# Repeated bias rows copied DRAM to DRAM in sixteen pieces, behind a modulation that begins one group earlier

## The chip, the cores and the metric

The kernel runs on one core of a Trainium2 chip. The metric is device time in microseconds for one execution; the time before is the median of three runs. The core has five engines that run instruction queues of their own: TensorE (PE, with its weight loads as PEld), VectorE (DVE), ScalarE (ACT), GpSimd (POOL) and SyncE (SP), which here issues all the DMAs. Every queue is worked off in order; an instruction that waits for a semaphore holds back what stands behind it on the same engine. The DMAs themselves run on sixteen DMA engines.

## The reference, cut to what matters

One layer of a streaming encoder on 1024 prompt frames and 32 sample frames, width 1024, in fp32:

```python
mod = jax.nn.silu(c) @ w_mod + b_mod                       # 9 vectors of 1024: shift, scale, gate for 3 sub-layers
h = adaln_in(x, gains[0], sh1, sc1)
x = x + 0.5 * g1 * rmsnorm(swiglu(h, w1_gate, w1_up, w1_down), gains[1])      # d_ff 2816
...
bias_a = rel_tab_a[:, clip(k - q, -128, 128) + 128]        # 8 heads
bias_b = t5_tab[:, t5_bucket(k - q)]                       # 8 heads
... attention with these biases, output projection, gate g2, then a second swiglu with g3
```

The change concerns two things that are needed late: the modulation vectors from number 2 on (first used when the first SwiGLU is complete), and the two bias tables, which the attention adds to its scores.

## The kernel before, in words

The first SwiGLU (`ffn("h1", ...)`, lines 516 to 597) works in 11 groups of two blocks of 128 hidden columns, x and y. For each of three blocks of frames (384, 384 and 288) a group computes `gate` and `up` for x and for y (24 matmuls of three terms for each product, in PSUM banks of which three rotate), the activation `sl` (ScalarE L541), its product with `up` (VectorE L542), a split into two parts `gg` (L544, L545) and the down projection `dn` of both, which is added to `facc` (L570, L572). The down projection of one block of frames runs between x and y of the next. The last three groups run their third block of frames at the end.

Every weight block of 512 KB is loaded by a DMA into `raw` (L292; three buffers, shared with the modulation's loads), and split there into two parts: ScalarE rounds it (L294), VectorE subtracts (L295). The loads for a group are issued during the group before it. ScalarE's splits stand in its queue between the `sl` of the running group, so a load that lands late holds back the next `sl`, and with it a PSUM bank that TensorE needs.

Side work is written as generators. `step(n)` runs the next pieces of the queue `side` and is called from inside the groups. The modulation is such a generator: `mod_aside(n)` (L215) loads one of 14 remaining chunks in four DMAs (L220), multiplies and adds on VectorE (L227, L229), and transposes the sums on TensorE into `pmt` (L239), which VectorE reduces into `modT` (L240). `mod_rest(gi)` (L625) is called at the end of group gi. After group 0 it called `bias_rows()` all at once; after group 1 it began the modulation.

`bias_rows()` (L251) loads both tables (L253, L258), lays each out on eight partitions, one head each, as 384 values (`ua`, `ubt`; 31 small copies at L261 for the second), and copies them to DRAM, each head's row 128 times over (L265): `skew_A` and `skew_B`, 8 x 128 x 384 values or 1.5 MB each. `bias_tiles` (L276) later reads them with a row step of 383 instead of 384, which shifts each row by one.

The order in which the DMAs stand on SyncE, and the instructions on the other engines, comes from a scheduler that simulates times while the program is built (from the end of group 0 on, for SyncE). DMAs use eight completion semaphores in turn, so one may have to wait for an earlier one that used the same.

Of the kernel before, what the change touches and what calls it, by code (L numbers as in the profile page):

```python
# [7 lines left out]
F32 = mybir.dt.float32  # L8
# [66 lines left out]
def encoder_step(ctx: ExitStack, tc, x_prompt, x_sample, cache_a_k, cache_a_v, cache_b_k, cache_b_v,  # L75
# [4 lines left out]
    te, ve, ae, ge, dma = nc.tensor, nc.vector, nc.scalar, nc.gpsimd, nc.sync  # L80
# [12 lines left out]
    dram = ctx.enter_context(tc.tile_pool(name="dram", bufs=1, space=DRAM))  # L93
# [12 lines left out]
    def s_tile(shape, name, dt=F32):  # L106
        return spool.tile(shape, dt, name=name, tag="s")
# [107 lines left out]
    def mod_aside(n):  # L215

        acc = [h_tile([128, 512], "macc") for _ in range(2)]
        for g in range(4):
            r = rpool.tile([128, 2, 512], F32, name="raw", tag="r")
            dma.dma_start(r, w_mod[0, 256 * g:256 * (g + 1), 512 * n:512 * (n + 1)]  # L220
                          .rearrange("(k p) n -> p k n", p=128))
            for kk in range(2):
                k = 2 * g + kk
                for j in range(2):
                    c = csil[:, k, j:j + 1]
                    if k == 0:
                        ve.tensor_scalar(acc[j], r[:, kk], c, None, op0=OP.mult)  # L227
                    else:
                        ve.scalar_tensor_tensor(acc[j], r[:, kk], c, acc[j], op0=OP.mult, op1=OP.add)  # L229
            yield  # L230
            yield
            yield
        yield
        yield
        c0 = 4 * n
        for j in range(2):
            pt = pc("pmt", (128, 4, 128))
            for b in range(4):
                te.transpose(pt[:, b, :], acc[j][:, 128 * b:128 * b + 128], ident)  # L239
            ve.tensor_reduce(modT[:, j, c0:c0 + 4], pt, axis=AX.X, op=OP.add)  # L240
        coefs(n)
        yield

    def mod_all(first, last):
        for n in range(first, last):
            yield from mod_aside(n)


    ub = {}

    def bias_rows():  # L251
        ta = s_tile([8, 257], "ta")
        dma.dma_start(ta, rel_bias_a[0])  # L253
        ua = s_tile([8, 384], "ua")
        ve.memset(ua[:, 0:128], 0.0)
        ve.tensor_scalar(ua[:, 128:384], ta[:, 0:256], ta[:, 0:1], None, op0=OP.subtract)
        tt = s_tile([8, 32], "tt")
        dma.dma_start(tt, t5_bias_table)  # L258
        ubt = s_tile([8, 384], "ubt")
        for lo, hi, b in T5_RANGES:  # L260
            ve.tensor_copy(ubt[:, lo + 255:hi + 256], tt[:, b:b + 1].to_broadcast([8, hi - lo + 1]))  # L261
        ve.memset(ubt[:, 383:384], 0.0)
        for kind, u in (("A", ua), ("B", ubt)):
            ub[kind] = dram.tile([8, 128, 384], F32, name="skew_" + kind)
            dma.dma_start(ub[kind], u[:, None, :].to_broadcast([8, 128, 384]))  # L265
        sk = consts.tile([128, 8], F32, name="sk")
        dma.dma_start(sk, bass.AP(tensor=sinks_b.tensor, offset=sinks_b.offset, ap=[[0, 128], [1, 8]]))
        sks = consts.tile([64, 4], F32, name="sks")
        for h in range(2):
            dma.dma_start(sks[32 * h:32 * h + 32], bass.AP(tensor=sinks_b.tensor, offset=sinks_b.offset + h,  # L270
                                                          ap=[[0, 32], [2, 4]]))
        nsk = consts.tile([128, 8], F32, name="nsk")
        ve.tensor_scalar(nsk, sk, -1.0, None, op0=OP.mult)
        ub["sk"], ub["sks"], ub["nsk"] = sk, sks, nsk
# [210 lines left out]
    def begin(key, gen, first=False):  # L485
        side.insert(0 if first else len(side), marked(key, gen))

    def marked(key, gen):
        yield from gen
        done.add(key)  # L490
# [5 lines left out]
    def between(f, tb, j, H):  # L496
        yield from resid(f, tb, j)
        dma.dma_start(xs_dram[j + 1][tb], f)
        yield from norm_h(f, tb, j + 1, H)
# [125 lines left out]
    def mod_rest(gi):  # L625
        if gi == 0:
            in_order.close()
            bias_rows()
        if gi == 1:
            begin("mod", mod_all(4, 18))  # L630

    ffn1 = ffn("h1", H1, F1, w1_gate, w1_up, w1_down, mod_rest, "h2", lambda tb: between(F1[tb], tb, 0, H2))
    first = start(0)
    for o in START:
# [713 lines left out]
```

## Time and profile before

| | |
|---|---|
| runs | 2225.36, 2229.99, 2230.26 us; median 2229.99 |
| the profiled execution | 2232.07 us, span 2230.3 us |
| mean granted clock of TensorE in it | 0.983 |
| busy in the span | TensorE 2163.1 us (97%), VectorE 1238.6 (56%), ScalarE 698.1 (31%), GpSimd 180.5 (8%) |
| DMA | 186.00 MB, mean 83 GB/s |

The first SwiGLU takes the time from 46 to about 840 us, the attention follows, and the second SwiGLU ends the program. To read it: TensorE is the engine that is busy nearly throughout, so the other engines' idle time says little by itself. What counts is where TensorE idles, who ended that, and at which clock it then runs. The groups can be told apart by the `sl` activations, six to a group; the first one (x, first frames) of groups 1 to 3 is at 124.25, 207.01 and 278.71 us.

### The profile page before, as it was taken

To read this page: it belongs to the slowest core of one execution; us is meant where nothing else is said; L and a number is where in the kernel's file an instruction comes from. 1 tells how busy PE (TensorE), PEld (TensorE's weight loads), DVE (VectorE), ACT (ScalarE), POOL (GpSimd) and SP (SyncE) were. 2 spreads that over 40 slices of the span, in tenths; PEclk is the share of its full clock that TensorE was granted. 3 is DMA by queue.
4 is the path that set the end of the run, shared out by engine and by line. 5 is a ranking of instruction groups with operands and counts; after the bars stand their busy time and mean duration, and the time that the engine had idled before them with its cause. 6 is when DMAs were issued, how large, how long until landed. Compare 5 with 4: busy or idle time off the path is not lost.

```text
span 2230.3 us, 33962 instructions
## 1 busy us (share of the span) xinstructions
PE 2163.1 (97%) x14012; PEld 2069.8 (93%) x14012; DVE 1238.6 (56%) x2425; ACT 698.1 (31%) x1450; POOL 180.5 (8%) x281
## 2 busy tenths in 40 slices
PE   6989999999999999899999899999999999999998
PEld 4989999999999999899788579999999999999998
DVE  5735677765643497677544775775433333333336
ACT  4411111111111253566544763433111111111133
POOL 2100000000000022100110413320000000000000
PEclk8999999999999999899999899999999999999999
DMA  9245344343321353110211221523211111111122
GB/s 328 85 76 125 105 122 132 104 123 95 104 76 57 90 162 121 59 31 20 68 30 30 77 59 56 161 81 104 85 57 39 44 43 47 57 38 55 41 67 81
DMA packets 200350, 186.00 MB, mean 83 GB/s; under 512 B 7340, under 2 KB 169540, under 8 KB 199044
## 3 DMA queue, kind: packets, MB, share of 16 engines
q1 hardware_dynamic: 200196, 183.84, 27.7%
q8 instruction: 110, 1.80, 0.3%
q14 instruction: 44, 0.36, 0.1%
HBM read 160.98 MB, written 22.84 MB: 82 GB/s over the span
## 4 chain that ended last, share of the span: by engine, by line
PE 84%; DMA 7%; DVE 6%; ACT 1%; issue 1%; POOL 1%; SPq 0%; DVEq 0%; ACTq 0%; POOLq 0%
PE dn L316 7%; PE up L316 7%; PE up L318 7%; PE up L317 7%; PE dn L317 7%; PE dn L318 7%; PE gate L318 7%; PE gate L317 7%; PE gate L316 7%; DMA raw<-in_w_up_dram 4%; PE po L705 3%; PE S L744 2%; PE pq L316 2%; PE pq L318 2%; PE pq L317 2%; PE pp L768 1%
## 5 line engine op out<-in xcount | busy, mean ns | idle before, releaser
L316 PE MATMUL up<-h_hi,w 128*128 128x384 f32 (+1 forms) x1056 | 341.1, 323 | 9.2 <-ACT sl L541 9.2
L316 PE MATMUL dn<-gg,w 128*128 128x384 f32 (+1 forms) x1056 | 340.8, 324 | 3.9 <-DVE facc L572 3.5
L317 PE MATMUL gate<-h_lo,w 128*128 128x384 f32 (+1 forms) x1056 | 340.1, 322 | 3.9 <-DVE h_lo L437 3.9
L316 PE MATMUL gate<-h_hi,w 128*128 128x384 f32 (+1 forms) x1056 | 341.2, 323 | 0.0
L317 PE MATMUL up<-h_lo,w 128*128 128x384 f32 (+1 forms) x1056 | 340.8, 323 | 0.0
L317 PE MATMUL dn<-gg,w 128*128 128x384 f32 (+1 forms) x1056 | 339.8, 322 | 0.6 <-DVE gg L545 0.6
L318 PE MATMUL up<-h_hi,w 128*128 128x384 f32 (+1 forms) x1056 | 340.4, 322 | 0.0
L318 PE MATMUL gate<-h_hi,w 128*128 128x384 f32 (+1 forms) x1056 | 340.4, 322 | 0.0
L318 PE MATMUL dn<-gg,w 128*128 128x384 f32 (+1 forms) x1056 | 339.4, 321 | 0.0
L572 DVE TENSOR_TENSOR facc<-dn,facc 128x768 f32<-128x768 f32 (+1 forms) x240 | 212.7, 888 | 221.4 <-PE dn L318 221.3
L295 DVE TENSOR_TENSOR w<-raw,w 128x1024 fp32r<-128x1024 f32 x187 | 232.3, 1250 | 170.7 <-ACT w L294 163.6
L294 ACT ACTIVATE w<-raw 128x1024 fp32r<-128x1024 f32 x187 | 195.8, 1056 | 278.0 <-PE dn L318 103.5
L541 ACT ACTIVATE sl<-gate 128x384 f32<-128x384 f32 (+1 forms) x132 | 60.9, 462 | 549.6 <-PE gate L318 549.5
L542 DVE TENSOR_TENSOR sl<-sl,up 128x384 f32<-128x384 f32 (+1 forms) x132 | 68.5, 519 | 282.3 <-PE up L318 282.0
L316 PEld LDWEIGHTS up<-h_hi,w 128*128 128x128 f32 x1056 | 199.1, 189 | 9.5 <-ACT sl L541 9.5
L316 PEld LDWEIGHTS dn<-gg,w 128*128 128x128 f32 x1056 | 198.7, 189 | 5.8 <-DVE facc L572 4.8
L317 PEld LDWEIGHTS gate<-h_lo,w 128*128 128x128 f32 x1056 | 198.7, 188 | 4.5 <-DVE h_lo L437 4.5
L317 PEld LDWEIGHTS dn<-gg,w 128*128 128x128 f32 x1056 | 198.7, 188 | 1.2 <-DVE gg L545 1.2
L318 PEld LDWEIGHTS up<-h_hi,w 128*128 128x128 f32 x1056 | 199.4, 189 | 0.0
L317 PEld LDWEIGHTS up<-h_lo,w 128*128 128x128 f32 x1056 | 199.2, 189 | 0.0
L316 PEld LDWEIGHTS gate<-h_hi,w 128*128 128x128 f32 x1056 | 198.9, 188 | 0.1
L318 PEld LDWEIGHTS gate<-h_hi,w 128*128 128x128 f32 x1056 | 198.7, 188 | 0.0
(224 smaller groups left out, 3365.3 us busy)
## 6 DMA issues: line engine op xcount, KB each, us to landing
raw<-in_w_mod_dram SPq DMA_DIRECT2D x56, 512.0 KB, 4.0
raw<-in_w_gate_dram SPq DMA_DIRECT2D x54, 512.0 KB, 3.9
raw<-in_w_up_dram SPq DMA_DIRECT2D x54, 512.0 KB, 4.6
raw<-in_w_down_dram SPq DMA_DIRECT2D x54, 512.0 KB, 4.5
raw<-in_w_in_dram SPq DMA_DIRECT2D x18, 512.0 KB, 5.0
wm<-in_w_mod_dram SPq DMA_DIRECT2D x8, 1024.0 KB, 7.8
raw<-in_w_out_dram SPq DMA_DIRECT2D x13, 512.0 KB, 4.4
xr<-xs SPq DMA_DIRECT2D x16, 384.0 KB, 3.3
```

Source lines behind the costliest of these rows:

```text
L294: ae.activation(w[:, 0], r, AF.Copy)
L295: ve.tensor_sub(w[:, 1], r, w[:, 0])
L316: te.matmul(ps, w[:, 0, k], hi, start=start, stop=False)
L317: te.matmul(ps, w[:, 0, k], lo, start=False, stop=False)
L318: te.matmul(ps, w[:, 1, k], hi, start=False, stop=stop)
L541: ae.activation(sl[:, :w], ps[0][:, :w], AF.Silu)
L542: ve.tensor_tensor(sl[:, :w], sl[:, :w], ps[1][:, :w], op=OP.mult)
L572: ve.tensor_tensor(o, ps[:, :, :w], o, op=OP.add)
L705: te.matmul(po[64 * h:64 * h + 64, :n], vsl(j, h, kn), PT(h, j, kn), start=j == 0, stop=j == nt - 1)
L744: te.matmul(S[:, c:ce], self.T[:, h, :], KQ[:, 0, 128 * k0 + c:128 * k0 + ce], start=True, stop=True)
L768: te.transpose(pp[:, j - j0, :], P[:, 128 * j:128 * j + 128], ident)
```

## The change

`bias_rows` becomes a generator. It first writes each table's eight rows to DRAM once (`rows_A`, `rows_B`, 12 KB each), and then issues sixteen copies from DRAM to DRAM, one for each table and head: one row of 1.5 KB is read 128 times into 128 consecutive rows. Between the pieces it yields. The modulation now begins after group 0, and the bias rows follow it in the same queue of side work.

```diff
         tt = s_tile([8, 32], "tt")
         dma.dma_start(tt, t5_bias_table)
+        yield
         ubt = s_tile([8, 384], "ubt")
...
+        rows = {}
         for kind, u in (("A", ua), ("B", ubt)):
+            rows[kind] = dram.tile([8, 384], F32, name="rows_" + kind)
+            dma.dma_start(rows[kind], u)
             ub[kind] = dram.tile([8, 128, 384], F32, name="skew_" + kind)
-            dma.dma_start(ub[kind], u[:, None, :].to_broadcast([8, 128, 384]))
+        yield
+        for kind in "BA":
+            for h in range(8):
+                yield
+                dma.dma_start(ub[kind][h], rows[kind][h:h + 1, :].to_broadcast([128, 384]))
+                yield
...
     def mod_rest(gi):
         if gi == 0:
             in_order.close()
-            bias_rows()
-        if gi == 1:
             begin("mod", mod_all(4, 18))
+            begin("bias", bias_rows())
```

Lines behind L258 move down by 9, behind the end of `mod_rest` by 8. On SyncE, where group 1 begins (raw are weights or modulation rows, told apart by the tensor they come from), there stood before:

```order
L292 DMA raw<-in_w_down_dram 128x1024 x2
L292 DMA raw<-in_w_gate_dram 128x8x128
L253 DMA ta<-in_rel_bias_a_dram 8x257
L258 DMA tt<-in_t_bias_table_dram 8x32
L265 DMA skew_A<-ua 1024x1x384
L292 DMA raw<-in_w_up_dram 128x8x128
L265 DMA skew_B<-ubt 1024x1x384
L292 DMA raw<-in_w_gate_dram 128x8x128
L292 DMA raw<-in_w_up_dram 128x8x128
L292 DMA raw<-in_w_down_dram 128x1024 x2
L220 DMA raw<-in_w_mod_dram 128x2x512 x10
```

The same place on SyncE in the changed kernel:

```order
L301 DMA raw<-in_w_down_dram 128x1024 x2
L220 DMA raw<-in_w_mod_dram 128x2x512 x10
L301 DMA raw<-in_w_gate_dram 128x8x128
L301 DMA raw<-in_w_up_dram 128x8x128
L301 DMA raw<-in_w_gate_dram 128x8x128
L301 DMA raw<-in_w_up_dram 128x8x128
L301 DMA raw<-in_w_down_dram 128x1024 x2
```

The copies are gone from here, and ten loads of the modulation stand ahead of group 2's weights; in the order of before that is so from the next group on. On VectorE, 13 operations of the modulation now stand ahead of the product of `sl` and `up` with which group 1 begins; before, it was 20 ahead of the one with which group 2 begins.

Six groups later on SyncE, in the changed kernel, behind the last modulation loads and group 7's gate and up weights:

```order
L301 DMA raw<-in_w_down_dram 128x1024
L253 DMA ta<-in_rel_bias_a_dram 8x257
L258 DMA tt<-in_t_bias_table_dram 8x32
L267 DMA rows_A<-ua 8x384
L301 DMA raw<-in_w_down_dram 128x1024
L273 DMA skew_A<-rows_A 128x384 x4
L267 DMA rows_B<-ubt 8x384
L273 DMA skew_A<-rows_A 128x384 x2
L273 DMA skew_B<-rows_B 128x384 x8
L273 DMA skew_A<-rows_A 128x384 x2
L301 DMA raw<-in_w_gate_dram 128x8x128
L301 DMA raw<-in_w_up_dram 128x8x128
```

Before, the two down loads were followed there by eight loads of the modulation and then by the gate and up loads of group 8. The sixteen pieces stand in one run, the gate and up loads of group 8 behind them. Each piece waits for its source row table and for the DMA issued eight before it, whose semaphore it takes over.

On ScalarE at group 7 the changed kernel has the splits of group 8's gate and up weights (`w_5419`, `w_5424`) ahead of the `sl` of y for the first frames (`sl_5060`):

```order
L550 ACTIVATE sl_4944<-gate_4892 128x384
L553 ACTIVATE gg_4947<-sl_4944 128x384
L303 ACTIVATE w_5419<-raw_5417 128x1024
L303 ACTIVATE w_5424<-raw_5422 128x1024
L550 ACTIVATE sl_5060<-gate_5008 128x384
```

Before, the same two splits (`w_5401`, `w_5406`) stood behind that `sl` (`sl_5003`):

```order
L541 ACTIVATE sl_4879<-gate_4815 128x384
L544 ACTIVATE gg_4882<-sl_4879 128x384
L541 ACTIVATE sl_5003<-gate_4947 128x384
L294 ACTIVATE w_5401<-raw_5399 128x1024
L294 ACTIVATE w_5406<-raw_5404 128x1024
```

The splits moved ahead by one `sl`. From the end of the first SwiGLU on, all five engines have the same order in both kernels, but for buffer numbers.

## Rows read from the trace of the kernel before

**Rows 1.** The page: its parts 1 and 4, busy time by engine, and the chain by engine.

```profile
PE 2163.1 (97%) x14012; PEld 2069.8 (93%) x14012; DVE 1238.6 (56%) x2425; ACT 698.1 (31%) x1450; POOL 180.5 (8%) x281
...
PE 84%; DMA 7%; DVE 6%; ACT 1%; issue 1%; POOL 1%; SPq 0%; DVEq 0%; ACTq 0%; POOLq 0%
```

**Rows 2.** Waits of TensorE, 100 to 880 us: us in total, times, longest.

```profile
PE up L316 <- ACT sl L541: 9.2, 1, 9.2
```

**Rows 3.** Windows of 10 us: busy of each engine, granted clock, DMA share, GB/s.

```profile
140.00:150.00 10.00, 7.18 (x42) 6.86 (x40) 0.00 (x0) 0.00 (x0) 0.00 (x0) 1.00 0.46 49
150.00:160.00 10.00, 3.65 (x11) 3.65 (x12) 2.25 (x3) 2.34 (x4) 0.00 (x0) 0.54 0.48 75
160.00:170.00 10.00, 10.00 (x56) 10.00 (x56) 3.03 (x4) 0.53 (x1) 0.00 (x0) 0.95 0.55 75
210.00:220.00 10.00, 8.44 (x56) 8.12 (x55) 10.00 (x17) 0.90 (x2) 0.00 (x0) 1.00 0.58 176
240.00:250.00 10.00, 9.30 (x54) 8.98 (x53) 6.95 (x10) 1.28 (x2) 0.00 (x0) 1.00 0.50 150
260.00:270.00 10.00, 10.00 (x66) 9.93 (x65) 8.57 (x14) 0.27 (x1) 0.00 (x0) 1.00 0.38 107
```

**Rows 4.** Timeline of ScalarE: start, us, instruction, idle before it and what ended it.

```profile
154.86 1.06 ACT L294 ACTIVATE w<-raw 128x1024 fp32r<-128x1024 f32 x1 [16.69 <-DMA raw<-in_w_up_dram]
155.82 0.47 ACT L541 ACTIVATE sl<-gate 128x384 f32<-128x384 f32 x1
```

**Rows 5.** Timeline of SyncE's DMA issues in the groups at 124 and 207.

```profile
112.89 0.38 SPq L292 DMA_DIRECT2D raw<-in_w_gate_dram  x1
...
118.44 0.82 SPq L265 DMA_DIRECT2D skew_A<-ua  x1
119.57 4.82 SPq L292 DMA_DIRECT2D raw<-in_w_up_dram  x1
124.44 21.45 SPq L265 DMA_DIRECT2D skew_B<-ubt  x1
...
191.09 33.54 SPq L220 DMA_DIRECT2D raw<-in_w_mod_dram  x10
...
261.23 37.53 SPq L220 DMA_DIRECT2D raw<-in_w_mod_dram  x10
```

**Rows 6.** Chain of work, 140 to 260 us: start, us, what.

```profile
119.57 35.20 DMA raw<-in_w_up_dram
...
157.03 0.32 PE up L317
...
161.56 0.17 PE up L317
```

**Rows 7.** DMA issues of the whole run: size, median us to landing.

```profile
raw<-in_w_mod_dram SPq DMA_DIRECT2D x56, 512.0 KB, 4.0
...
out_dram<-vt SPq DMA_DIRECT2D x2, 512.0 KB, 2.9
...
out_dram<-kr SPq DMA_DIRECT2D x4, 256.0 KB, 2.5
```

**Rows 8.** DMA queue, 140 to 150 us: packets, MB, share of 16 engines.

```profile
q1 hardware_dynamic: 321, 0.49, 46.2%
```

**Rows 9.** Timeline of ScalarE: the first sl of three groups.

```profile
124.25 0.49 ACT L541 ACTIVATE sl<-gate 128x384 f32<-128x384 f32 x1 [2.70 <-PE gate L318]
...
207.01 0.47 ACT L541 ACTIVATE sl<-gate 128x384 f32<-128x384 f32 x1
...
278.71 0.50 ACT L541 ACTIVATE sl<-gate 128x384 f32<-128x384 f32 x1 [2.07 <-PE gate L318]
```

**Rows 10.** Timeline of SyncE: the down loads of the last modulated group, and the next gate load.

```profile
519.04 24.93 SPq L292 DMA_DIRECT2D raw<-in_w_down_dram  x2
...
577.21 0.37 SPq L292 DMA_DIRECT2D raw<-in_w_gate_dram  x1
```

**Rows 11.** Timeline of ScalarE in that group: the sl of y.

```profile
575.42 0.49 ACT L541 ACTIVATE sl<-gate 128x384 f32<-128x384 f32 x1 [2.87 <-PE gate L318]
```

## The prediction

> **What bounds the kernel now.** The page comes first: TensorE is busy for 97% of the span, and the chain that ended last is 84% TensorE and 7% DMA [rows 1]. So a gain has to come from microseconds in which TensorE idles or runs at a low clock, and the waits of TensorE are the second view. Between 100 and 880 us, the stretch in which the change moves anything, one wait stands out: the up matmul waits 9.2 us, once, for ScalarE's sl [rows 2]. The windows show where: TensorE is busy 7.18 us of 140 to 150 and 3.65 us of 150 to 160, and after that idle stretch the granted clock is 0.54 and then 0.95, where all other rows shown have 1.00 [rows 3]. ScalarE's timeline names the cause. The sl at 155.82 runs directly behind a weight split (L294), and that one idled 16.69 us for the DMA of the up weights [rows 4]. SyncE's timeline says why that load was late: it is issued at 119.57, right behind skew_A (118.44), the copy of ua to 128 repeated rows per head [rows 5], and it lands 35.20 us later [rows 6], where a 512 KB load otherwise takes about 4 [rows 7]. Last comes the DMA view while only these copies run: q1 moves 321 packets in the 10 us from 140 to 150 and takes 46.2% of sixteen engines [rows 8]. That is 7.4 engines busy, and 7.4 x 10 / 321 = 0.23 us for a packet of 1.5 KB. One skew copy is 1024 packets, 128 on each of eight engines, so 128 x 0.23 = 29.5 us: the extra 31 us of the up load. The load has parts on all sixteen engines and waits for the eight that are taken.
>
> [...]
>
> **The change part by part.** Where both numberings differ, lines are those of before. I count against the profiled execution, 2232.07 us (span 2230.3), which lies 2.08 us above the median of 2229.99.
>
> 1. The two copies leave the first group. SyncE's order there goes from the down loads straight to the modulation's loads, so nothing is left that could hold the next weights for 31 us. What goes is TensorE's idle stretch, (10 - 7.18) + (10 - 3.65) = 9.17 us [rows 3], and the slow stretch behind it. From 156.3, where the sl of rows 4 is done, a matmul takes 0.32 us, and at 161.56 0.17 [rows 6]: some 5.2 us at half speed, hence 2.6 us lost. Together -11.8 us.
>
> 2. The modulation (14 chunks, four loads of 512 KB each) begins one group earlier. Its work on VectorE and TensorE stays the same in amount, so as work it costs nothing; it leaves the last group that had it and enters the group that starts with the sl at 124.25 [rows 9]. What matters is how well its first group runs. In before that is the group with sl at 207.01, and it shows two small idle stretches of TensorE, 1.56 us (210 to 220) and 0.70 us (240 to 250), while the group after has none at 260 to 270 [rows 3]. In the changed kernel the group at 207 is an ordinary one, so -2.3 us. In exchange the group at 124 becomes the first. Its first modulation load can be issued at 112.9, where SyncE issued the gate load [rows 5], 11.4 us ahead of the sl at 124.25. In before the lead was 207.01 - 191.09 = 15.9 us, and in the next group 278.71 - 261.23 = 17.5 us [rows 5, 9]. The smaller lead delays VectorE: its in-order queue holds 13 modulation operations ahead of the product sl x up of that first block, each waiting for its load. Against that, 20 stand there in the group at 207. Bounds: nothing, as at 260 to 270; or worse than the 2.3 of rows 3. The slope of the two leads known is 2.3 us lost for 1.6 us of lead; 4.5 us less lead would then be 2.3 + 6.4 = 8.7 us. The row nearest in kind is the first group of before with its 2.3, which has more modulation work in front but more lead: I take +3.
>
> 3. The sixteen pieces. They are issued beside the last modulated group's end, behind the second down load. In before that pair of loads ends issuing at 519.04 + 24.93 = 544 [rows 10], so at about 533 in the new time. All sixteen stand on SyncE in one run, ahead of the next group's gate and up loads; the yields between them do not spread them. ScalarE splits those two weights ahead of the sl that ran at 575.42 in before [rows 11], that is 564. TensorE can still do an up chain and a gate chain behind that block's gate, 24 matmuls of 0.17 us each or 8 us together, and ScalarE needs two splits of 1.06 us: the up weights must land by about 570. No row shows a DRAM to DRAM copy, so two bounds. I count sixteen engines for a piece with 128 outer rows, since the copy with eight outer rows kept 7.4 busy; if it stays on eight, the price is that of rival C. With the packet time of rows 8, 2048 packets on sixteen engines are 128 x 0.23 = 29.5 us, to 562; two 512 KB loads at some 4 us each behind them [rows 7] make 571, and TensorE idles 1 us, or 3 with a late start. From the other side, a 512 KB store of 1 KB rows lands in 2.9 us [rows 7], 3 MB at that rate take 17 us, and 550 + 8 = 558 is early enough. The source in DRAM relieves the eight SBUF rows that were read 128 times each; nothing there gives a gain beyond item 1. Nearest in packet size is rows 8, nearest in engines the store: I take +0.5, with 0 and 3 as ends. The extra copies rows_A and rows_B are 12 KB each; SyncE waits for rows_A on VectorE's ua, but the down load queued behind it waits for its buffer until later anyway. The bias tables' small VectorE copies are the same in both kernels, and the bias tiles are read only in the attention: 0.
>
> 4. From the last pieces on, the orders of all engines are the same as before apart from buffer numbers: 0.
>
> [...]
>
> Sum: -11.8 - 2.3 + 3 + 0.5 = -10.6 us, of the profiled execution 2221.5 us, or 2219.4 against the median. I forecast **2219 us**; with the ends of items 2 and 3 (0 to 8.7, and 0 to 3) it runs from 2215.9 to 2227.6.
>
> **Rivals.**
>
> A. The modulation's first group gives most of it back (item 2 at 8.7 us): -11.8 - 2.3 + 8.7 + 0.5 = -4.9, 2225 us. For it: the lead of 11.4 us, and loads that share three buffers with the down weights, so that VectorE must wait for most of them. Against: the fewer operations ahead of the first sl, and a VectorE that is busy 0.00 to 3.03 us of ten between 140 and 170, where it was 10.00 of ten at 210 to 220 [rows 3].
>
> B. The pieces go one behind another. Eighteen copies at the 2.5 us of rows 7 are 45 us: 533 + 45 + 8 = 586, 16 us behind 570, and 2.6 us of low clock as in item 1; -10.6 - 0.5 + 18.6 = +7.5, 2237 us. It decides against the change from 11 us of idle and slow time on, hence when the pieces need over about 36 us. Against: on SyncE a piece waits, besides its source, only for the DMA eight before it, and rows 5 show the modulation's loads overlapping, ten in 33.54 us with VectorE as their brake.
>
> C. The engines read the same 1.5 KB of DRAM 128 times, and this is slower than reading it from SBUF. At twice the packet time of rows 8 the pieces take 59 us, to 592; the up weights land at 600, 30 us late: -11.1 + 30 + 2.6 = +21.5, 2251 us. It turns the sign from 0.28 us a packet on. For it: no row shows such reads. Against: in rows 8 only eight rows of SBUF fed everything, which is as narrow a source.
>
> D. The load was late for another reason than the skew copies, and the idle stretch stays: 2230 us. Against it stands the arithmetic of rows 8, 29.5 of 31 us.
>
> **How the numbers follow.** Chances: forecast 68%, A 14%, B 6%, C 7%, D 5%. The bound of what this kernel's runs can tell from no change is 0.3%, 6.7 us: faster means below 2223.3. The forecast case gives faster in nine of ten, A, D and the rest give no change, B and C slower (B in nearly all). That is 0.64 and a few hundredths from the better half of A, so 0.68 faster, 0.20 same, 0.12 slower. The range reaches from 2213 (item 2 at 0 and the runs' spread of some 3 us) to 2230, and leaves out B and C.
>
> **What would show it.** Right: at 140 to 160 TensorE busy 20 of 20 and granted clock 1.00; up loads of the first groups landing in 4 to 5 us; the distance between the sl at 124.25 and its successor of the next group about 72 to 75 us instead of 82.8 [rows 9]; the DMA share while the pieces run near 0.9 instead of 0.46, for 15 to 30 us. Item 2 is wrong if TensorE idles over 5 us in total between 115 and 195. Item 3 is wrong if a weight split of ScalarE waits for a DMA at 560 to 600 and TensorE idles behind it. The forecast fails altogether if the pieces need over 36 us, or if the idle stretch at 147 stays.

## The result, and the profile after

The changed kernel takes 2215.21 us (median, 2211.38 to 2217.6), the kernel before 2228.52 us in runs beside it (2225.36 to 2230.26): ratio 0.994, 95% interval [0.992, 0.996]. The forecast was 2219 us. The profiled execution took 2217.6 us, 14.5 less than that of before.

The page's first line and the waits of TensorE between 100 and 880 us answer to [rows 1, 2]:

```profile
PE 2161.6 (98%) x14012; PEld 2068.6 (93%) x14012; DVE 1239.1 (56%) x2425; ACT 697.8 (31%) x1450; POOL 179.2 (8%) x281
```

```profile
PE dn L325 <- DVE facc L581: 1.0, 1, 1.0
PE dn L326 <- DVE gg L554: 0.6, 1, 0.6
```

TensorE's work is the same to 2 us. The wait of 9.2 us is gone, and nothing over 1.0 us has come in its place. The windows (columns as in [rows 3]) show TensorE without idle and at a granted clock of 1.00, where rows 3 had 7.18, 3.65, 8.44 and 9.30 of ten, and 0.54 for the clock:

```profile
140.00:150.00 10.00, 10.00 (x60) 10.00 (x59) 9.18 (x15) 1.02 (x2) 0.00 (x0) 1.00 0.40 109
150.00:160.00 10.00, 10.00 (x62) 9.94 (x61) 7.74 (x12) 2.53 (x3) 0.00 (x0) 1.00 0.53 153
...
210.00:220.00 10.00, 10.00 (x61) 9.97 (x60) 9.84 (x17) 1.54 (x3) 0.00 (x0) 1.00 0.47 149
240.00:250.00 10.00, 10.00 (x71) 10.00 (x71) 5.86 (x9) 3.26 (x5) 0.00 (x0) 1.00 0.18 55
```

ScalarE's first sl of groups 1 and 2 answers to [rows 9]: 70.87 us apart, where it was 82.76. In group 1, now the modulation's first, VectorE's product of that sl and up ends behind its 13 operations at 129.72 + 0.55:

```profile
123.87 0.49 ACT L550 ACTIVATE sl<-gate 128x384 f32<-128x384 f32 x1 [2.39 <-PE gate L327]
...
194.74 0.49 ACT L550 ACTIVATE sl<-gate 128x384 f32<-128x384 f32 x1 [2.24 <-PE gate L327]
```

```profile
125.08 4.72 DVE L229 SCALAR_TENSOR_TENSOR macc<-raw,csil,macc 128x512 f32<-128x512 f32 x7
129.72 0.55 DVE L551 TENSOR_TENSOR sl<-sl,up 128x384 f32<-128x384 f32 x1
```

At the pieces' new place, SyncE's timeline (start, us, what) answers to [rows 10], and the DMA view of 531 to 553 us to [rows 8]:

```profile
530.60 2.49 SPq L273 DMA_DIRECT2D skew_A<-rows_A  x4
...
537.75 4.95 SPq L273 DMA_DIRECT2D skew_B<-rows_B  x8
542.74 1.24 SPq L273 DMA_DIRECT2D skew_A<-rows_A  x2
544.08 0.54 SPq L301 DMA_DIRECT2D raw<-in_w_gate_dram  x1
544.72 1.47 SPq L301 DMA_DIRECT2D raw<-in_w_up_dram  x1
```

```profile
q1 hardware_dynamic: 5401, 5.17, 85.2%
...
skew_A<-rows_A SPq DMA_DIRECT2D x8, 192.0 KB, 5.4
skew_B<-rows_B SPq DMA_DIRECT2D x8, 192.0 KB, 4.6
```

All sixteen pieces and the weight loads among them, 5.17 MB, pass in these 22 us on 85% of the sixteen engines; a piece lands 5 us after its issue, so the pieces overlap. While pieces run alone (540 to 544 us) the DMA view shows:

```profile
DMA packets 702, 0.96 MB, mean 241 GB/s; under 512 B 74, under 2 KB 702, under 8 KB 702
q1 hardware_dynamic: 702, 0.96, 84.0%
```

That is 16 x 0.84 x 4 / 702 = 0.077 us a packet, or 0.086 if the 74 short ones took no time: well under half of the 0.23 us of [rows 8]. Behind them ScalarE's split of the next weights waits for TensorE and not for a load:

```profile
563.31 2.01 ACT L303 ACTIVATE w<-raw 128x1024 fp32r<-128x1024 f32 x2 [7.53 <-PE dn L327]
565.23 0.47 ACT L550 ACTIVATE sl<-gate 128x384 f32<-128x384 f32 x1
```

### The profile page after: what moved, and what is told of

It is laid out like the page before. It is cut to its first block, busy times and chain, and to the rows that moved or that the text cites. A ratio compares the mean times of both kernels' runs of the same rounds, so it can differ in the third digit from the quotient of the medians.

```text
span 2215.8 us, 33976 instructions
## 1 busy us (share of the span) xinstructions
PE 2161.6 (98%) x14012; PEld 2068.6 (93%) x14012; DVE 1239.1 (56%) x2425; ACT 697.8 (31%) x1450; POOL 179.2 (8%) x281
## 4 chain that ended last, share of the span: by engine, by line
PE 90%; DVE 4%; DMA 3%; ACT 1%; issue 1%; POOL 0%; SPq 0%; ACTq 0%; DVEq 0%; POOLq 0%
PE dn L325 7%; PE dn L326 7%; PE dn L327 7%; PE gate L327 7%; PE gate L326 7%; PE up L327 7%; PE up L326 7%; PE gate L325 7%; PE up L325 7%; PE po L713 3%; PE S L752 2%; PE pq L325 2%; PE pq L327 2%; PE pq L326 2%; DMA raw<-in_w_gate_dram 1%; PE pp L776 1%
## 5 line engine op out<-in xcount | busy, mean ns | idle before, releaser
L325 PEld LDWEIGHTS dn<-gg,w 128*128 128x128 f32 x1056 | 199.2, 189 | 1.6 <-DVE facc L581 1.2
L326 PEld LDWEIGHTS dn<-gg,w 128*128 128x128 f32 x1056 | 199.2, 189 | 1.0 <-DVE gg L554 0.9
L327 PEld LDWEIGHTS dn<-gg,w 128*128 128x128 f32 x1056 | 199.1, 189 | 0.0
```

The costliest lines, as they stand in the source:

```text
L325: te.matmul(ps, w[:, 0, k], hi, start=start, stop=False)
L326: te.matmul(ps, w[:, 0, k], lo, start=False, stop=False)
L327: te.matmul(ps, w[:, 1, k], hi, start=False, stop=stop)
```

## The experiments

Diffs are against the changed kernel unless said otherwise; times are medians, and ratios are to the kernel before with their 95% intervals.

**The changed kernel again**, no edit: 2214.87 us, 0.9934 [0.9921, 0.9947]. So a difference below some 3 us between the variants says nothing.

**Which part is needed: the modulation's earlier start?**

```diff
         if gi == 0:
             in_order.close()
+        if gi == 1:
             begin("mod", mod_all(4, 18))
             begin("bias", bias_rows())
```

> The other half: the pieces behind the modulation as in the change, but the modulation begins after group 1 as before. Nothing at all is copied in group 1. Theory T: no idle stretch at 147. If the small idle stretches of the modulation's first group (2.3 us before) belong to a late start of its loads behind the old copies, they go too and the time is the changed kernel's within 1 us; if every first group of the modulation has them, or if the earlier start is worth something by itself, 2 to 4 us more than the changed kernel and 1 to 3 us of idle TensorE between 195 and 250.

Measured: 2213.6 us, 0.9936 [0.9923, 0.9948]. TensorE's waits at 100 to 880 us add up to 2.1 us, none over 1.0. The earlier start is worth nothing. Here the modulation first runs in group 2, as before, and TensorE no longer has the small idles that it had there.

**The place behind the modulation?** The pieces go back to the first group, the modulation again begins after it:

```diff
         if gi == 0:
             in_order.close()
+            for _ in bias_rows():
+                pass
+        if gi == 1:
             begin("mod", mod_all(4, 18))
-            begin("bias", bias_rows())
```

> Half of the change: the sixteen pieces from DRAM, but all at the old place behind group 0, and the modulation begins after group 1 as before. Theory T with short copies: in the changed kernel the pieces and three loads took 22 us at 531 to 553, so here the next weights land at most some 15 us late, less than the 22 us of slack which the 31 us of the old copies exceeded by 9; no idle stretch at 147, time as the changed kernel's or up to 2.3 us above it (2215 to 2218). Rival R1 (the gain comes from the modulation's earlier start or from taking the copies out of the first group, whatever their form): the idle stretch stays at least in part, 2222 to 2229.

Measured: 2216.21 us, 0.9942 [0.9929, 0.9954], no idle of TensorE over 0.6 us. The place isn't needed either. One thing moved with it: the up load of group 2 stood ahead of the pieces on SyncE (119.17), not behind the first.

**The sixteen engines?** One DMA per table, its eight heads outermost, from DRAM:

```diff
-            for h in range(8):
-                yield
-                dma.dma_start(ub[kind][h], rows[kind][h:h + 1, :].to_broadcast([128, 384]))
-                yield
+            yield
+            dma.dma_start(ub[kind], rows[kind][:, None, :].to_broadcast([8, 128, 384]))
+            yield
```

> Place as in the change, source in DRAM, but one copy per table with the eight heads outermost instead of sixteen pieces. Theory S (a packet read from DRAM is short, about 0.09 us by the changed kernel's trace, 702 packets in 540 to 544 at 84% of sixteen engines; the old 0.23 us belonged to eight SBUF rows): 256 packets on each of eight engines take 22 us, DMA share about 0.5, no idle TensorE, 2215 us. Rival E (what matters is the sixteen engines, a packet takes 0.2 us from anywhere): 50 to 60 us, the next gate and up weights land after 585, TensorE idles 12 us or more at 570 to 590, 2228 us or more.

Measured: 2216.76 us, 0.9949 [0.9935, 0.9962], no idle over 1.0 us. On half the engines (a share of 0.53 at 193 GB/s from 532 to 536 us) each copy takes some 11 us instead of the 31 of the kernel before. So neither the cutting nor the count of engines is what made the copies harmless.

**The old copies at the new place.** The two copies of the kernel before, read from SBUF, behind the modulation that begins after group 0 (against the kernel before):

```diff
         dma.dma_start(tt, t5_bias_table)
+        yield
...
         if gi == 0:
             in_order.close()
-            bias_rows()
-        if gi == 1:
             begin("mod", mod_all(4, 18))
+            begin("bias", bias_rows())
```

> The place alone: the modulation begins in the first group and the two old copies (from the eight SBUF rows, the eight heads outermost) stand behind it, at about 526 to 535 us, skew_A ahead of the last modulated group's second down load, skew_B behind that one and ahead of the next gate and up loads. Theory S (the copies are slow by their source: 0.23 us for a packet of 1.5 KB, some 31 us each, and whatever stands behind them waits): skew_A from 526, the down load behind it lands near 557 to 560; gate and up land near 590 where they are needed by about 565 to 570; TensorE idles 15 to 30 us once or twice between 555 and 600, and the kernel takes 2230 to 2245 us, nothing gained against the kernel before. Theory P (what counted was only that the copies left the crowded first group, whatever they read): no idle of TensorE over 2 us, 2213 to 2217 us.

Measured: 2244.67 us, 1.0066 [1.0049, 1.0083], slower than before. TensorE's waits, and ScalarE's splits that idled for a load:

```profile
PE up L317 <- ACT sl L542: 11.4, 1, 11.4
PE dn L317 <- ACT gg L545: 8.2, 1, 8.2
```

```profile
560.09 1.06 ACT L295 ACTIVATE w<-raw 128x1024 fp32r<-128x1024 f32 x1 [21.81 <-DMA raw<-in_w_down_dram]
...
591.91 1.06 ACT L295 ACTIVATE w<-raw 128x1024 fp32r<-128x1024 f32 x1 [28.11 <-DMA raw<-in_w_gate_dram]
```

The stall of before appears twice, once behind each copy. The new place alone makes the kernel slower. The kernel just above it has the same two copies at the same place, but from DRAM, and takes some 27 us less: at this place the source is what counts.

**The source alone.** Against the kernel before: its place, its two copies, from row tables in DRAM:

```diff
+            row = dram.tile([8, 384], F32, name="rows_" + kind)
+            dma.dma_start(row, u)
             ub[kind] = dram.tile([8, 128, 384], F32, name="skew_" + kind)
-            dma.dma_start(ub[kind], u[:, None, :].to_broadcast([8, 128, 384]))
+            dma.dma_start(ub[kind], row[:, None, :].to_broadcast([8, 128, 384]))
```

> The source alone: the kernel before, its two copies with the eight heads outermost at their place in the first groups and the modulation begun one group later, but read from row tables in DRAM. Through that the order of SyncE changes as well: the up load of group 2 stands ahead of skew_A, and the next gate load ahead of skew_B. Theory S: each copy takes about 11 us (as with eight engines from DRAM behind the modulation) and not 31; no idle of TensorE over 2 us between 100 and 260, 2213 to 2217 us. Rival P: the copies still collide with the weights there; TensorE idles 5 to 10 us, 2222 to 2230 us.

Measured: 2212.52 us, 0.9932 [0.991, 0.9955], no idle over 0.8 us: the whole gain, by two added lines and a changed one. The DMA queue from 131 to 136 us (skew_B alone; packets, MB, share):

```profile
q1 hardware_dynamic: 613, 0.94, 51.8%
```

That is 16 x 0.518 x 5 / 613 = 0.068 us a packet and 188 GB/s, again on some eight engines (16 x 0.518 = 8.3). But SyncE's order had changed too: the up load ahead of skew_A, the next gate load ahead of skew_B. The next kernel keeps that order and goes back to SBUF.

**That order, the old source** (against the source-alone kernel):

```diff
+            back = s_tile([8, 384], "back_" + kind)
+            dma.dma_start(back, row)
-            dma.dma_start(ub[kind], row[:, None, :].to_broadcast([8, 128, 384]))
+            dma.dma_start(ub[kind], back[:, None, :].to_broadcast([8, 128, 384]))
```

> The order of the source-alone kernel with the old source: the row tables go to DRAM and back into eight SBUF rows, and the two copies read these, so that the up load of group 2 stands ahead of skew_A as it does there. Theory S (the source): the copies take 31 us each again, skew_A to about 153, skew_B to about 183; the up load behind skew_B is issued near 148 and lands near 180 where it is needed near 160: TensorE idles 10 to 25 us between 150 and 185, 2228 to 2240 us. Rival O (the order: all that hurt was the one up load behind skew_A): no idle over 2 us, 2213 to 2217 us.

Measured: 2235.64 us, 1.0031 [1.0017, 1.0045]. ScalarE's split of the up weights behind skew_B, a wait of TensorE and the DMA queue from 148 to 156 us:

```profile
193.48 1.06 ACT L298 ACTIVATE w<-raw 128x1024 fp32r<-128x1024 f32 x1 [17.44 <-DMA raw<-in_w_up_dram]
```

```profile
PE dn L320 <- DVE facc L576: 16.5, 5, 12.8
```

```profile
q1 hardware_dynamic: 275, 0.40, 45.6%
```

0.21 us a packet and 50 GB/s again, and 23 us between two kernels that differ by the source (and the 12 KB trip back). Rival O falls. The split came 13 us later than I put it. Besides the 12.8 us TensorE lost 2.6 at 157, behind an sl for which the trace names skew_A's landing. In the kernel's text `sl` and `back_A` come out of one pool of five buffers (`s_tile`), so this sl probably took over the buffer from which skew_A still read; no run tests that.

**Engines or rows of SBUF?** The sixteen pieces, each from one SBUF row, on sixteen engines:

```diff
-        rows = {}
+        us = {"A": ua, "B": ubt}
...
-            rows[kind] = dram.tile([8, 384], F32, name="rows_" + kind)
-            dma.dma_start(rows[kind], u)
...
-                dma.dma_start(ub[kind][h], rows[kind][h:h + 1, :].to_broadcast([128, 384]))
+                dma.dma_start(ub[kind][h:h + 1], us[kind][h:h + 1, None, :].to_broadcast([1, 128, 384]))
```

> The sixteen pieces at the changed kernel's place, 128 rows outermost on sixteen engines, but read from one SBUF row each and not from DRAM. If the limit of the old copies was that of each engine or packet (0.23 us a packet on each engine), sixteen engines need 2048 / 16 x 0.23 = 29.5 us for all, from about 530 to 562: TensorE idles 0 to 4 us, 2214 to 2219 us. If it was that of the eight rows of SBUF together (49 GB/s for 1.5 MB in 31 us), 3.1 MB need 64 us when pieces of several heads overlap: the next up weights land near 600, TensorE idles about 30 us, 2240 to 2250 us. If it is a limit of each single row, 49 / 8 = 6 GB/s and 32 us a piece when pieces of one head go one after another, it is between 64 us (eight in flight) and 512 us: TensorE idles from 30 to some 480 us, 2245 to 2700 us.

Measured: 2283.5 us, 1.0248 [1.0227, 1.027]. TensorE's wait, then windows, and the DMA view of 580 to 600 us:

```profile
PE up L323 <- ACT sl L548: 65.0, 1, 65.0
```

```profile
590.00:600.00 10.00, 0.00 (x0) 0.00 (x0) 0.00 (x0) 0.00 (x0) 0.00 (x0) 0.50 0.79 35
600.00:610.00 10.00, 0.00 (x0) 0.00 (x0) 0.00 (x0) 0.00 (x0) 0.00 (x0) 0.50 0.88 27
...
630.00:640.00 10.00, 2.83 (x9) 2.83 (x10) 3.48 (x4) 3.40 (x5) 0.00 (x0) 0.50 0.73 202
```

```profile
q1 hardware_dynamic: 498, 0.68, 82.5%
```

Sixteen busy engines move 34 GB/s and then 27, less than eight did (49), and a packet takes 16 x 0.825 x 20 / 498 = 0.53 us on the mean. The 34 hold a short rise, 54 GB/s from 588 to 592; from 580 to 588 and from 600 to 620 the rate is 27. The source sets the rate, then, and not the engines: from DRAM the same pieces moved 241 GB/s with 84.0% of the engines busy. The 0.23 us of [rows 8] was no price of an engine: the copy from DRAM took 0.068 on as many.

**Any SBUF source?** The row goes from DRAM to 128 SBUF rows, and the piece from there:

```diff
-                dma.dma_start(ub[kind][h], rows[kind][h:h + 1, :].to_broadcast([128, 384]))
+                wide = s_tile([128, 384], "wide")
+                dma.dma_start(wide, rows[kind][h:h + 1, :].to_broadcast([128, 384]))
+                dma.dma_start(ub[kind][h], wide)
```

> Each piece goes by way of SBUF: the row of a head is first copied from DRAM into a tile of 128 SBUF rows, and the piece is stored from there, so that every one of its 128 packets reads another SBUF row. Same size, same number of rows and same sixteen engines as the pieces that read one SBUF row; twice the DMA traffic of the changed kernel, and SyncE's order is mixed with the next weights. Theory S in its narrow form (slow is the repeated reading of few SBUF rows): a store takes 2 to 6 us to land, as the pieces from DRAM, and packets in such a stretch 0.06 to 0.1 us; 2213 to 2222 us. Rival: slow is any SBUF source with packets of 1.5 KB in this pattern: packets of 0.2 us and more, stores of over 10 us each, the weights behind them late, 2235 us and more.

Measured: 2216.03 us, 0.9948 [0.9932, 0.9964]. The same 192 KB land in 1.9 us from 128 rows (3.1 for skew_A); in the kernel with one-row pieces (second fence) they took ten times that, waiting for each other included:

```profile
skew_B<-wide SPq DMA_DIRECT2D x8, 192.0 KB, 1.9
```

```profile
skew_B<-ubt SPq DMA_DIRECT2D x8, 192.0 KB, 23.2
```

**Single rows, or neighbours?** The kernel with the old source and the new order, its eight rows four SBUF rows apart:

```diff
-            back = s_tile([8, 384], "back_" + kind)
+            wide = s_tile([32, 384], "back_" + kind)
+            back = wide.rearrange("(h f) n -> h f n", f=4)[:, 0, :]
```

> As the kernel with the row tables taken back into SBUF and the up load ahead of skew_A, but the eight rows of a table lie four SBUF rows apart (0, 4, ... 28) and not next to each other (0 to 7). With adjacent rows the copy ran at 50 GB/s, 0.21 us a packet. Theory R (each row, read again and again, gives only 50 / 8 = 6 GB/s): nothing changes, 31 us a copy, TensorE idles about 16 us, 2235 us. Theory N (neighbouring rows share a way out of SBUF, and rows 0 to 7 had two such ways of some 25 GB/s each): eight ways, up to 8 x 25 = 200 GB/s, which is what eight engines got from DRAM; packets of 0.06 to 0.08 us, a copy in 8 to 12 us, no idle of TensorE over 3 us, 2212 to 2219 us. [...]

Measured: 2216.16 us, 0.9939 [0.9924, 0.9954], no idle over 0.6 us. And eight apart (the same edit with 64 and f=8):

> The same with the rows eight apart (0, 8, ... 56). Theory R: 50 GB/s and 2235 us again. Theory N in the plain form that only direct neighbours share: as with rows four apart, near 200 GB/s. [...]

Measured: 2216.4 us, 0.9938 [0.9921, 0.9955], no idle over 0.7 us. The DMA queue with one copy alone on it, from 136.2 to 137.9 us (rows four apart) and from 124 to 127 us (eight apart):

```profile
q1 hardware_dynamic: 222, 0.34, 53.1%
```

```profile
q1 hardware_dynamic: 200, 0.31, 50.0%
```

The first is 0.065 us a packet and 222 x 1536 bytes / 1.7 us = 200 GB/s, the second 0.12 us and 102 GB/s; adjacent rows gave 50, in a kernel that differs from these two by the rows alone. Theory R falls: it wants 50 three times. For rows four apart N's figures came out, 200 GB/s and 0.065 us in 0.06 to 0.08. That only direct neighbours share falls, since eight apart is half as fast as four apart (102 against 200), and no run shows why. The two ways of 25 GB/s that N gives to rows 0 to 7 were an estimate; 27 GB/s for the one-row pieces against 50 for eight adjacent rows fit it, but no run counts the ways. The 200 GB/s may also be the limit of the engines and not of the source: on some eight engines the copy from DRAM got 188. What the short rise to 54 GB/s was isn't shown.

**How much room had the pieces?** Every piece twice, the second into tables that nobody reads:

```diff
+            ub2[kind] = dram.tile([8, 128, 384], F32, name="twin_" + kind)
...
                 dma.dma_start(ub[kind][h], rows[kind][h:h + 1, :].to_broadcast([128, 384]))
+                dma.dma_start(ub2[kind][h], rows[kind][h:h + 1, :].to_broadcast([128, 384]))
```

> The changed kernel with every piece issued a second time right behind itself, into twin tables that nothing reads: 32 pieces, 6.2 MB, at the same place behind the modulation. It measures the slack of item 3. The sixteen pieces of the changed kernel took 22 us (531 to 553) with three weight loads among them; by that, 32 take about 40 us, from 529 to 569, and the gate and up loads queued behind them land at about 573 to 580, where they are needed by about 570. Theory S: ScalarE's weight split waits for a DMA there, TensorE idles 2 to 10 us near 570, 2217 to 2227 us. If the need was put too early in the prediction, or later pieces go faster alone, no idle and 2213 to 2217 us. If pieces go one behind another (rival B), over 60 us: TensorE idles over 20 us, 2237 us and more.

Measured: 2217.08 us, 0.9947 [0.993, 0.9963]. ScalarE's splits behind the pieces, and TensorE's wait:

```profile
569.41 1.06 ACT L305 ACTIVATE w<-raw 128x1024 fp32r<-128x1024 f32 x1 [14.78 <-DMA raw<-in_w_gate_dram]
571.07 1.06 ACT L305 ACTIVATE w<-raw 128x1024 fp32r<-128x1024 f32 x1 [0.60 <-DMA raw<-in_w_up_dram]
```

```profile
PE up L327 <- ACT sl L552: 0.3, 1, 0.3
```

Now the splits do wait for the loads. The up weights are there at 571.07 and TensorE idles 0.34 us: the need lies at 570.7, where the prediction had 570. Twice the traffic just fits; the idle is less than the 2 us at the low end of theory S.

## Why the prediction was right, and where it was not

1. *The copies leave group 1, -11.8.* Confirmed: TensorE is busy 20 of 20 at clock 1.00, and every kernel without slow copies anywhere is 11 to 17 us faster than before. The cause named, a weight load held up behind a slow copy, is confirmed by the kernels that keep the slow copies, behind the modulation or in group 1 behind the up load: the stall comes back at the load behind the copy (ScalarE's splits idle 21.81 and 28.11 us, and 17.44). Rival D falls.

2. *The small idles go, -2.3; the new first modulated group costs +3.* The first half holds, the second is the step that failed: TensorE idles 0 where I put 3. I had taken the 2.3 us for a cost of the modulation's first group and scaled it by the lead of its loads. With the modulation in the same group but no slow copies before it, the idle isn't there. So it was an aftermath of the slow copies. How their lateness reached the dn that idled isn't followed here, but ScalarE's timeline of before shows the gate split ahead of that group still waiting for its load:

```profile
187.02 1.06 ACT L294 ACTIVATE w<-raw 128x1024 fp32r<-128x1024 f32 x1 [3.71 <-DMA raw<-in_w_gate_dram]
```

Slope and lead were no measure: the modulation's first loads were issued at 112.51, which is the predicted lead of 123.87 - 112.51 = 11.4 us, and nothing idled behind it.

```profile
112.51 30.92 SPq L220 DMA_DIRECT2D raw<-in_w_mod_dram  x10
```

For the same reason the groups lie 70.87 us apart, below the 72 to 75 that were to show it. What I had set against the smaller lead, the 13 operations in place of 20, came true: from the start of sl to that of its product it takes 129.72 - 123.87 = 5.9 us, against 216.59 - 207.01 = 9.6 in the first modulated group of before. Its product in VectorE's timeline:

```profile
216.59 0.55 DVE L542 TENSOR_TENSOR sl<-sl,up 128x384 f32<-128x384 f32 x1
```

But it wasn't needed either. In the kernel with the late modulation the 20 operations stand there again, the product comes 199.91 - 191.72 = 8.2 us behind its sl, and TensorE doesn't wait at all from 100 to 260 us:

```profile
191.72 0.49 ACT L550 ACTIVATE sl<-gate 128x384 f32<-128x384 f32 x1 [1.24 <-PE gate L327]
```

```profile
199.91 0.55 DVE L551 TENSOR_TENSOR sl<-sl,up 128x384 f32<-128x384 f32 x1
```

Rival A falls with its price.

3. *The sixteen pieces, +0.5 (0 to 3).* 0. Window (22 us, in 17 to 30), DMA share (0.85, near 0.9) and need (570) came out. The packet price did not: 0.077 to 0.086 us, not 0.23. I had read 0.23 us as the time of a packet on its engine; it was the time of the source, eight adjacent SBUF rows (from rows four apart 0.065 us, from DRAM 0.068, on as many engines). That +0.5 came out near 0 all the same was luck: at 0.23 us a packet the 29.5 us would nearly have fitted too, and so the error stayed hidden. In the same sentence as rival C ("as narrow a source") stood the wrong picture: DRAM rows read 128 times each fed 241 GB/s, eight adjacent rows of SBUF 49. C falls, and so does B: the pieces overlap, sixteen with medians of 4.6 and 5.4 us in 22 us.

4. *The rest, 0.* TensorE's other waits and its busy time agree to 2 us.

With 0 for the two costs the sum is -14.1 us; the profiled executions differ by 14.5, the medians by 13.3. One sum among the chances was off: nine of ten of the forecast's 0.68 are 0.61, not 0.64. No term of the time rests on it.

What the prediction didn't see is that its two reasons, place and cutting, were each unnecessary: the kernel gains through DRAM as the source (2212.52 us), or through other SBUF rows (2216.16 and 2216.4). At the new place the old source would have cost 15 us instead of giving 13.

## What to carry over

Where a DMA with few, long packets shows a share of the engines that doesn't fit its rate (here 46.2% for 49 GB/s, where DRAM as the source had 51.8% for 188), divide: share x engines x time / packets is the packet's time, and if it is far above that of other DMAs with such packets (0.23 us against 0.068), look at the end that is narrow before cutting the DMA or moving it. A cost seen once behind a disturbance (the 2.3 us) is no price of what runs there; look for the next occurrence without the disturbance. And a change that moves, cuts and reroutes at once should be run in its parts: here one of the three carried all.

## What the runs showed of the hardware

The same eight-row broadcast, 1.5 MB with 46 to 53% of the sixteen engines busy, ran at 49 to 50 GB/s from SBUF rows 0 to 7, 102 from rows eight apart, 200 from rows four apart and 188 from DRAM. More engines with a single row for each copy were slower still: 27 GB/s for most of the time, with 0.88 of sixteen engines busy (600 to 610). A row of DRAM read again and again was no such brake: under 0.09 us a packet with 84.0% of sixteen engines busy, and 241 GB/s. And in the windows from 580 to 630, in which TensorE waited for those pieces and ran nothing, its granted clock read 0.50, and still 0.50 in the window in which it began again (630 to 640).
